# Moving ten convolution taps from GpSimd and ScalarE to VectorE in a two-layer decoder trunk

## The chip, the core and the metric

The kernel runs as one program on one NeuronCore of a Trainium2 chip. The number that counts is the device time of one execution in microseconds (us); lower is better. The engines go by their profile names: PE (matrix products) with PEld (its weight loads), DVE (VectorE), ACT (ScalarE), POOL (GpSimd) and SP (which issues most DMAs).

## What is computed

Two layers (`DEPTH = 2`) over 512 tokens of width 1024, in float32. Each layer is a half-weighted SwiGLU, a mixer, and a second half-weighted SwiGLU. The mixer is the part that matters here:

```python
h = rms_norm(x, mix_norm[l])
a, g, q, k, v = jnp.split(h @ w_in[l], splits, axis=-1)
conv_out = conv_module(a, g, conv_w[l], conv_b[l], conv_norm[l])
...
diff_out = diff_attention(q, k, v, rel_bias, lam, lam_init, subln_norm[l])
x = x + jnp.concatenate([conv_out, diff_out], axis=-1) @ w_out[l]

def conv_module(a, g, conv_w, conv_b, conv_norm):
    u = a * jax.nn.sigmoid(g)
    y = lax.conv_general_dilated(u, rhs, window_strides=(1,), padding=[(CONV_K - 1, 0)], ...)
    y = y + conv_b
    return jax.nn.silu(rms_norm(y, conv_norm))
```

The convolution is causal and depthwise: each of 512 channels is the weighted sum of 31 shifted copies of itself (`CONV_K = 31`). Its RMS norm runs over all 512 channels, so no channel can be finished before the sums of all of them are there. The attention has 4 heads with two softmax maps each, swept over four blocks of 128 queries.

## The kernel before

Activations lie feature-major: 128 features on the partitions, 512 tokens along the row. Large products are made of float32 parts, a rounded high part and the rest (`whi`/`wlo` for weights, `acth`/`actl` for activations), three products for each; ACT makes the high part of a weight (line 101) and DVE or POOL the rest (line 102).

`mixer` runs once per layer. Its 512 convolution channels are four tiles of 128, numbered 0 to 3. The order in which the source states the work is: the input projection of tiles 0 to 2 (`conv_in`), the query and key projections, tile 3's input projection, then two attention steps and the value projections, then `conv_taps(c, POOL_TAPS[c])` for the four tiles, then the other fourteen attention steps, then `conv_finish`, then the output projection. This order is a priority; a planner with its own costs for each instruction lays the final order of every engine at build time, and it may put later work ahead of earlier work that it does not see ready. On the chip each engine then runs its list in order.

`conv_taps(c, n)` makes tile `c`. The first `n` taps are ACT products (`prod`, line 916, two buffers) that POOL adds up one after the other (`yp`, lines 912 and 917); the others are DVE multiply-adds, each of which reads the running sum in a PSUM bank (`ps_y`) and one shifted slice of the input `u` in SBUF and writes the sum back (line 931). Where both have a share, DVE adds them (line 934). Then ACT squares the tile (`csq`, line 903; `csum`, line 900, for tile 0) and POOL adds the square to `csum` (line 904). Before the change tiles 0 and 2 are all DVE's (31 taps each), tile 1 is all POOL's and ACT's (31), and tile 3 is split: 10 to POOL and ACT, 21 to DVE.

```python
if n:
    yp = mp.tile([P, SEQ], F32, tag="yp%d" % (n < TAPS), name="yp")
    G.tensor_scalar(yp, us[c][:, 0:SEQ], ...)                        # line 912
    for t in range(1, n):
        p = mt.tile([P, SEQ], F32, tag="prod", name="prod")
        S.activation(p, us[c][:, t : t + SEQ], AF.Copy, scale=...)   # line 916
        G.tensor_tensor(yp, yp, p, op=ALU.add)                       # line 917
...
for t in range(n + 1 if n else 1, TAPS):
    V.scalar_tensor_tensor(ys[c] if last else y, us[c][:, t : t + SEQ], ..., y, ...)  # line 931
if n:
    V.tensor_tensor(ys[c], y, yp, op=ALU.add)                        # line 934
conv_square(c, ys[c])
```

`conv_finish` turns `csum` into one factor per token (PE transposes on line 267, DVE lines 271 and 272, POOL line 260, DVE line 289, PE line 293, ACT line 298), and for each tile runs POOL line 942, ACT 944, DVE 945, ACT 946, DVE 947. What it writes is the convolution half of the output projection's input.

An attention step is one head of one block of 128 queries; steps go from the last block (rows 512 wide) to the first (128 wide). `softmaxes` makes two score maps on PE (line 962, PSUM tags `sc` and `po`, two banks each), adds the bias and finds the maximum on DVE (line 966), takes the exponential on ACT (line 970), and combines the maps on DVE (lines 973, 975, 976). Two steps later `keys_first` transposes the map on PE (line 983) and copies it on ACT (line 985); one more step later `values` multiplies it with the values on PE (line 992). After four heads come a normalisation (lines 999 to 1007) and `block_out` (PE line 1019, ACT 1021, DVE 1022), which writes the attention half of the output projection's input. The output projection (lines 200, 203, 204, 1069) uses the tags `sc` and `po` too; it states the attention half for tokens 256 to 511 first, then the convolution half for all tokens, then the attention half for tokens 0 to 255. All 12 products of a 128-feature output need either the four convolution tiles or the attention blocks of their tokens.

Of the kernel before, what the change touches and what calls it, by code (L numbers as in the profile page):

```python
# [29 lines left out]
TAPS = 31  # L30
# [19 lines left out]
)  # L50
ORDER = (0, 4, 1, 5, 2, 6, 3, 7)

POOL_TAPS = (0, TAPS, 0, 10)


_COLS = [
# [14 lines left out]
def trunk(ctx: ExitStack, tc: tile.TileContext, xt, par, lamv, relb, onehot,  # L71
# [717 lines left out]
    def mixer(l, pr, after, begun):  # L789
        with tc.tile_pool(name="mix", bufs=1) as mp, tc.tile_pool(name="mt", bufs=2) as mt:  # L790
# [115 lines left out]
            def conv_taps(c, n):  # L906

                wc = _AT["conv_w"] + c * TAPS
                yp = None
                if n:  # L910
                    yp = mp.tile([P, SEQ], F32, tag="yp%d" % (n < TAPS), name="yp")
                    G.tensor_scalar(yp, us[c][:, 0:SEQ], pars[l][:, wc : wc + 1], col(l, "conv_b", c),
                                    op0=ALU.mult, op1=ALU.add)
                    for t in range(1, n):
                        p = mt.tile([P, SEQ], F32, tag="prod", name="prod")
                        S.activation(p, us[c][:, t : t + SEQ], AF.Copy, scale=pars[l][:, wc + t : wc + t + 1])  # L916
                        G.tensor_tensor(yp, yp, p, op=ALU.add)  # L917
                if n == TAPS:
                    ys[c] = yp
                    conv_square(c, yp)  # L920
                    return
                y = bank("y", "ps_y")
                if not n:
                    V.tensor_scalar(y, us[c][:, 0:SEQ], pars[l][:, wc : wc + 1], col(l, "conv_b", c),
                                    op0=ALU.mult, op1=ALU.add)
                else:
                    V.tensor_scalar(y, us[c][:, n : n + SEQ], pars[l][:, wc + n : wc + n + 1], None, op0=ALU.mult)
                ys[c] = us[c][:, PAD:]
                for t in range(n + 1 if n else 1, TAPS):
                    last = t == TAPS - 1 and not n  # L930
                    V.scalar_tensor_tensor(ys[c] if last else y, us[c][:, t : t + SEQ],
                                           pars[l][:, wc + t : wc + t + 1], y, op0=ALU.mult, op1=ALU.add)
                if n:
                    V.tensor_tensor(ys[c], y, yp, op=ALU.add)
                conv_square(c, ys[c])
# [116 lines left out]
            for c in range(CT):  # L1052
                conv_taps(c, POOL_TAPS[c])
            for n in range(2, len(steps) + 5):
# [139 lines left out]
```

## Time and profile before

| what | value |
|---|---|
| median of 3 runs | 1769.95 us (1769.82 to 1770.12) |
| profiled execution, its own time | 1770.11 us |
| its span in the profile | 1768.3 us (1.8 us lie outside it) |
| granted TensorE clock | 0.999 |
| mixer's convolution and attention, layer 0 | about 365 to 515 us of the span |
| the same in layer 1 | about 1243 to 1393 us |

"Busy" counts the time in which at least one instruction of an engine runs. PE matmuls are pipelined and their drawn ends reach into the next one, so PE can look busy across a short wait. In a timeline row the first number is the start, the second the length, "xN" the number of instructions merged into the row, and the brackets give the idle time before it and what ended it.

### The profile page before, as it was taken

The numbers are of one execution on the slowest core, as the hardware profiler recorded it, in microseconds if no ns is written. First come the engines' busy times: TensorE is split into PE (matmuls) and PEld (weight loads), VectorE is DVE, ScalarE is ACT, GpSimd is POOL, SyncE is SP. The second block draws the span as 40 slices with busy tenths as digits, with TensorE's granted clock in tenths as the row PEclk, the third lists the DMA queues.
The fourth block names the chain that finished last, engine by engine and source line by source line (L and its number), as shares of the span: only waits on it lengthen the run. The fifth ranks groups of instructions, "written<-read, shape, count | busy, mean of one in ns | idle before, by whom it ended". The sixth has DMA issues, their size and how long they took to land.

```text
span 1768.3 us, 32976 instructions
## 1 busy us (share of the span) xinstructions
PE 1757.9 (99%) x11852; PEld 1620.9 (92%) x11852; DVE 1474.8 (83%) x2655; ACT 1035.9 (59%) x1955; POOL 514.2 (29%) x497
## 2 busy tenths in 40 slices
PE   9999999999999999999999999999999999999998
PEld 7799999988788899999988999999887888999998
DVE  7969888987877969889987798899878678698887
ACT  6546566755855436566644565666559554465664
POOL 1011112169960011212200121121898600111122
PEclk9999999999999999999999999999999999999999
DMA  7457677533223457787544577776231335577775
GB/s 229 129 139 188 167 190 189 141 117 102 66 78 114 126 130 176 172 196 180 141 143 110 150 176 173 200 162 172 90 109 49 94 103 138 131 179 177 192 184 130
DMA packets 166613, 257.78 MB, mean 146 GB/s; under 512 B 19271, under 2 KB 63318, under 8 KB 166448
## 3 DMA queue, kind: packets, MB, share of 16 engines
q1 hardware_dynamic: 129600, 201.25, 36.3%
q0 software_dynamic: 36416, 54.12, 19.3%
q8 instruction: 93, 1.52, 0.4%
q14 instruction: 72, 0.59, 0.1%
q10 hardware_dynamic: 432, 0.29, 0.1%
HBM read 253.48 MB, written 3.42 MB: 145 GB/s over the span
## 4 chain that ended last, share of the span: by engine, by line
PE 93%; ACT 2%; POOL 1%; DVE 1%; DMA 0%; issue 0%; DVEq 0%; POOLq 0%; ACTq 0%
PE ps_pair L437 36%; PE ps_pair L526 18%; PE ps_pair L200 9%; PE ps_pair L203 9%; PE ps_pair L204 9%; PE ps_pair L845 2%; PE ps_pair L847 2%; PE ps_pair L846 2%; PE ps_out L200 2%; PE ps_out L203 2%; PE ps_out L204 2%; POOL yp L917 1%; ACT e L970 1%; ACT ps_sc L970 1%; ACT prod L916 0%; ACT at L985 0%
## 5 line engine op out<-in xcount | busy, mean ns | idle before, releaser
L101 ACT ACTIVATE whi<-wraw 128x512 fp32r<-128x512 f32 x744 | 453.2, 627 | 375.9 <-PE ps_pair L203 162.8
L102 DVE TENSOR_TENSOR wlo<-wraw,whi 128x512 fp32r<-128x512 f32 x640 | 426.2, 685 | 105.4 <-ACT whi L101 100.8
L160 POOL DMA_DIRECT2D wsum<-in_gu x128 | 111.9, 910 | 698.0 <-DMA wsum<-in_gu 291.9
L437 PE MATMUL ps_pair<-acth,wlo 128*128 128x256 f32 x1024 | 289.8, 283 | 0.0
L437 PE MATMUL ps_pair<-actl,whi 128*128 128x256 f32 x1024 | 289.8, 283 | 0.0
L437 PE MATMUL ps_pair<-acth,whi 128*128 128x256 f32 x1024 | 289.8, 283 | 0.0
L437 PE MATMUL ps_pair<-th,whi 128*128 128x256 f32 x768 | 217.3, 283 | 0.0
L437 PE MATMUL ps_pair<-tl,whi 128*128 128x256 f32 x768 | 217.3, 283 | 0.0
L437 PE MATMUL ps_pair<-th,wlo 128*128 128x256 f32 x768 | 217.3, 283 | 0.0
L203 PE MATMUL ps_pair<-actl,whi 128*128 128x512 f32 x512 | 199.7, 390 | 0.0
L200 PE MATMUL ps_pair<-acth,whi 128*128 128x512 f32 x512 | 199.0, 391 | 0.3 <-DVE gs L656 0.3
L204 PE MATMUL ps_pair<-acth,wlo 128*128 128x512 f32 x512 | 199.2, 390 | 0.0
L437 PEld LDWEIGHTS ps_pair<-actl,whi 128*128 128x128 f32 x1024 | 196.6, 192 | 0.2
L437 PEld LDWEIGHTS ps_pair<-acth,whi 128*128 128x128 f32 x1024 | 196.6, 192 | 0.2
L437 PEld LDWEIGHTS ps_pair<-acth,wlo 128*128 128x128 f32 x1024 | 196.6, 192 | 0.0
L160 POOL DMA_DIRECT2D wsum<-in_dn x112 | 98.8, 1107 | 271.2 <-ACT keep L442 51.0
L102 POOL TENSOR_TENSOR wlo<-wraw,whi 128x512 fp32r<-128x512 f32 x104 | 136.4, 1332 | 38.2 <-ACT whi L101 30.6
L437 PEld LDWEIGHTS ps_pair<-th,whi 128*128 128x128 f32 x768 | 147.5, 192 | 0.0
L437 PEld LDWEIGHTS ps_pair<-tl,whi 128*128 128x128 f32 x768 | 147.5, 192 | 0.0
L437 PEld LDWEIGHTS ps_pair<-th,wlo 128*128 128x128 f32 x768 | 147.5, 192 | 0.0
L526 PE MATMUL ps_pair<-hh,whi 128*128 128x256 f32 x512 | 144.9, 283 | 0.0
L526 PE MATMUL ps_pair<-hl,whi 128*128 128x256 f32 x512 | 144.9, 283 | 0.0
(210 smaller groups left out, 4448.8 us busy)
## 6 DMA issues: line engine op xcount, KB each, us to landing
wraw<-in_gu SPq DMA_DIRECT2D x280, 256.0 KB, 3.5
wsum<-in_gu SPq DMA_DIRECT2D x128, 256.0 KB, 3.8
wsum<-in_gu POOLq DMA_DIRECT2D x128, 256.0 KB, 4.9
wraw<-in_dn SPq DMA_DIRECT2D x68, 256.0 KB, 3.4
wraw<-in_wqkv SPq DMA_DIRECT2D x48, 256.0 KB, 2.8
wraw<-in_wout SPq DMA_DIRECT2D x48, 256.0 KB, 2.7
wraw<-in_dn SPq DMA_DIRECT2D x64, 128.0 KB, 3.9
wraw<-in_wag SPq DMA_DIRECT2D x32, 256.0 KB, 3.0
```

The costliest lines, as they stand in the source:

```text
L101: S.activation(hi, raw, AF.Copy)
L102: (eng or V).tensor_tensor(out=lo, in0=raw, in1=f32(hi), op=ALU.subtract)
L160: nc.gpsimd.dma_start(dst[:, to], src, accum_op=ALU.add)
L200: first = T.matmul(ps, wh, xh, start=start, stop=False)
L203: T.matmul(ps, wh, xl, start=False, stop=False)
L204: T.matmul(ps, wl, xh, start=False, stop=stop)
L437: mm = T.matmul(ps, l, r, start=first and i == j == 0, stop=False, skip_group_check=True)
L526: mm = T.matmul(ps, s[:, f], r, start=side not in self.begun, stop=False, skip_group_check=True)
L845: T.matmul(ps[n], xh[:, t], wh, start=k == 0, stop=False)
L846: T.matmul(ps[n], xh[:, t], wl, start=False, stop=False)
L847: T.matmul(ps[n], xl[:, t], wh, start=False, stop=k == KT - 1)
L970: S.activation(e, e, AF.Exp, bias=mn, scale=-1.0, accum_out=sm[:, m, h : h + 1])
```

## The change

Tile 3's ten POOL and ACT taps become DVE taps. Nothing else is edited. In each layer POOL loses one line-912 instruction and nine line-917 additions, ACT loses nine line-916 products, and DVE has 31 tap instructions for tile 3 (one line 924, thirty line 931) in place of 21 (one line 927, twenty line 931) and the addition of line 934. Tile 1 stays with POOL and ACT. The planner lays the order anew.

```diff
-POOL_TAPS = (0, TAPS, 0, 10)
+POOL_TAPS = (0, TAPS, 0, 0)
```

## The prediction

> **What bounds the kernel now.** I read the page's busy times and chain shares first.
>
> ```profile
> PE   1757.9 (99%) x11852; PEld 1620.9 (92%) x11852; DVE 1474.8 (83%) x2655; ACT 1035.9 (59%) x1955; POOL 514.2 (29%) x497
> PE 93%; ACT 2%; POOL 1%; DVE 1%; DMA 0%; issue 0%; DVEq 0%; POOLq 0%; ACTq 0%
> ```
>
> PE carries 93% of the chain that ended last, so over the whole kernel a change on the other engines can only win or lose what PE waits. The chain leaves PE for long only in the two mixers, so I asked for busy times by stretch there: first the time in which DVE runs tile 3's taps, then a gap on DVE, then the attention steps to the start of the output projection, then its first microseconds. Columns: stretch and its length, then PE, PEld, DVE, ACT, POOL busy.
>
> ```profile
> 443.44:464.22 20.78, 20.78 (x90) 15.98 (x89) 19.51 (x35) 15.96 (x31) 18.59 (x16) 1.00 0.09 27
> 464.22:466.49 2.27, 2.27 (x10) 1.54 (x9) 0.00 (x2) 2.27 (x5) 2.27 (x3) 1.00 0.22 75
> 466.49:475.00 8.51, 8.51 (x38) 5.18 (x37) 6.79 (x21) 7.76 (x21) 8.51 (x8) 1.00 0.44 136
> 475.00:485.00 10.00, 9.69 (x68) 8.26 (x66) 8.98 (x32) 9.97 (x30) 9.38 (x9) 1.00 0.26 79
> 485.00:495.30 10.30, 9.31 (x62) 7.51 (x63) 10.03 (x38) 7.74 (x28) 3.74 (x5) 1.00 0.01 2
> 495.30:505.00 9.70, 8.97 (x73) 8.63 (x72) 8.69 (x30) 8.78 (x24) 9.07 (x8) 1.00 0.09 28
> ```
>
> PE's visible idle in layer 0 is 0.31 + 0.99 + 0.73 = 2.03 us, all after 475. Up to 475 PE has no visible gap. From 475 to 485 ACT is full (9.97 of 10.00), from 485 to 495.3 DVE is (10.03 of 10.30). DVE's own idle is 1.27, 2.27, 1.72, 1.02 and 0.27 us in the first five stretches: 6.55 us in all. Layer 1 repeats this, so I work one layer out and double it:
>
> ```profile
> 1362.90:1373.20 10.30, 9.30 (x61) 7.50 (x62) 10.03 (x37) 7.74 (x27) 3.86 (x5) 1.00 0.01 2
> 1373.20:1382.90 9.70, 8.94 (x73) 8.63 (x72) 8.69 (x30) 8.78 (x25) 8.96 (x8) 1.00 0.08 27
> ```
>
> **What leaves POOL and ACT.** The rows of the tiles `u` and `yp` give count, then min/median/max in ns:
>
> ```profile
> L916 ACT ACTIVATE prod<-u,par x78: 704/722/746, 375.7 to 1359.9; 128x512 f32<-128x512 f32 x78
> L931 DVE SCALAR_TENSOR_TENSOR ps_y<-u,par,ps_y x156: 743/756/758, 369.7 to 1341.3; 128x512 f32<-128x512 f32 x156
> L934 DVE TENSOR_TENSOR u<-ps_y,yp x2: 680/680/681, 484.8 to 1362.8; 128x512 f32<-128x512 f32 x2
> L945 DVE SCALAR_TENSOR_TENSOR u<-th,u x6: 690/1337/1780, 498.5 to 1387.1; 128x512 f32<-128x512 f32 x6
> ```
>
> ```profile
> L917 POOL TENSOR_TENSOR yp<-yp,prod x78: 1266/1296/1337, 376.9 to 1361.0; 128x512 f32<-128x512 f32 x78
> L912 POOL TENSOR_SCALAR yp<-u,par x4: 770/782/817, 376.1 to 1323.2; 128x512 f32<-128x512 f32 x4
> ```
>
> POOL loses 9 x 1.30 + 0.78 = 12.5 us per layer, ACT loses 9 x 0.72 = 6.5 us. In the stretch where ACT is full, two things follow: attention's exponentials come sooner, and no product waits for a POOL buffer. Neither is worth anything by itself if DVE, which feeds ACT, has no time left. I therefore value the relief only as idle time that DVE can now fill. None of these instructions issues a DMA or is waited for by a queue that does, save POOL's weight splits of line 102, which move up.
>
> **What DVE gets.** The price of a tap depends on its neighbours:
>
> ```profile
> 452.78 0.75 DVE L931 SCALAR_TENSOR_TENSOR ps_y<-u,par,ps_y 128x512 f32<-128x512 f32 x1
> 453.44 0.69 DVE L966 CUSTOM_DVE_ANT_0 ps_sc<-ps_sc,bias 128x512 f32<-128x512 f32 x1
> ...
> 461.10 3.12 DVE L931 SCALAR_TENSOR_TENSOR ps_y<-u,par,ps_y 128x512 f32<-128x512 f32 x4
> 466.49 0.69 DVE L966 CUSTOM_DVE_ANT_0 e<-ps_sc,bias 128x512 f32<-128x512 f32 x1 [2.27 <-PE ps_sc L962]
> ...
> 471.39 0.75 DVE L976 SCALAR_TENSOR_TENSOR e<-ps_sc,c,e 128x512 f32<-128x512 f32 x1
> ...
> 484.80 0.68 DVE L934 TENSOR_TENSOR u<-ps_y,yp 128x512 f32<-128x512 f32 x1
> ...
> 494.56 0.74 DVE L1022 SCALAR_TENSOR_TENSOR actl<-ps_o,gsub,acth 128x512 fp32r<-128x512 f32 x1
> ```
>
> Taps that wait for each other step by (3.12 - 0.75) / 3 = 0.79 us; a tap with another instruction behind it takes 453.44 - 452.78 = 0.66 us. The twenty-first tap ends at 464.22, and DVE then stands for 2.27 us until PE has the next scores. Three of the ten new taps fit there (3 x 0.79 = 2.4). The other seven mix with the 512-wide attention steps, as taps did from 452 on: 7 x 0.66 = 4.6. Line 934 goes (0.68). DVE's net gain in work is 2.4 + 4.6 - 0.7 = 6.3 us per layer; the bounds are 10 x 0.66 - 0.68 = 5.9 and 10 x 0.79 - 0.68 = 7.2.
>
> Against it stand the idle times. The 2.27 us are filled whole. Of the 1.72 us to 475 DVE waits for scores that PE makes in its own time, so I credit half, 0.86. Of the 1.02 + 0.27 us to 495.3 some is waiting for ACT, which has lost products there; half again, 0.65. The 1.27 us before 464.22 lie ahead of the new taps and count nothing. Room: 3.8 us. So `block_out` of the second block, whose last instruction started at 494.56, comes 6.3 - 3.8 = 2.5 us late. Bounds: if all of the later idle time were used, 5.9 - 5.28 = 0.6; if only the gap, 7.2 - 2.27 = 4.9.
>
> PE's rows say who feels this:
>
> ```profile
> 474.59 0.60 PE L983 MATMUL ps_at<-ident,e 128*128 128x128 f32 x4
> ...
> 488.88 0.60 PE L267 MATMUL ps_rows<-ident,csum 128*128 128x128 f32 x4
> ...
> 495.65 0.36 PE L200 MATMUL ps_out<-acth,whi 128*128 128x256 f32 x1
> ...
> 498.69 0.39 PE L962 MATMUL ps_sc<-kt,qz 128*128 128x128 f32 x2
> ...
> 503.69 0.47 PE L200 MATMUL ps_out<-acth,whi 128*128 128x512 f32 x1 [0.73 <-DVE r L973]
> ```
>
> The third step's map was ready at 471.39 + 0.75 = 472.14 and PE transposed it at 474.59: 2.4 us of slack, which covers the early steps. In the narrow steps after 485 there is no such slack, since PE already stood still 0.99 us there. The output projection's first matmul, at 495.65, followed the `block_out` at once.
>
> **What moves with it.** Tile 3 was complete at 484.80 + 0.68 = 485.48. Its 31st tap should now end near 466.5 plus seven taps mixed with seven other instructions, 7 x (0.66 + 0.66) = 9.2, so near 476. `conv_finish` can start nine microseconds earlier. That has two sides. Its DVE instructions come into the fully used stretch before 495: I count two of the eight of lines 945 and 947 ahead of `block_out`, 2 x 0.69 = 1.4 us of further lateness (0.69 is line 945 at its shortest; at its longest, 1.78, it would be 3.6). And it hands PE convolution-half products while attention is slow: I credit the 0.73 us at 503.69 and the 0.99 us before 495.3. Per layer: 2.5 + 1.4 - 0.73 - 0.99 = 2.2 us lost. Twice that is 4.4 us on the profiled execution's 1770.11, so 1774.5; the median of the runs lies 0.16 below that execution, so 1774.3.
>
> [...]
>
> **The rivals.**
>
> First, **faster: the convolution half becomes PE's filler.** The chain of waits, in order of time, ran over POOL's taps and ACT's products into the attention steps:
>
> ```profile
> 458.59 2.56 POOL yp L917 x2
> ...
> 474.70 0.61 ACT prod L916
> ...
> 480.87 0.61 ACT prod L916
> ```
>
> If `conv_finish` is through by about 490, PE can work on the convolution half (8 outputs of twelve 512-wide matmuls each) whenever attention stalls. It decides if the first such matmul, at 503.69 before, starts before about 492. For it: tile 3 is ready nine microseconds sooner, and PE has 2.03 us of visible gaps, with more hidden under drawn matmul ends. Against it: `conv_finish` ranks behind the attention steps in the source, it needs a DVE that is full, and the output projection shares its four PSUM banks with scores, the last of which came only at 498.69. If the visible gaps go and half as much hidden time with them, the gain is near 2.5 us a layer (2.03 + 1.0, less 0.5 of early lateness): 1765. Both layers at twice the visible gap, 8 us, is the end I can see: 1762.
>
> Second, **no change worth measuring.** The slack of 2.4 us takes the lateness, ACT's relief lets DVE use all its later idle time, and the two sides of `conv_finish` cancel: 0.6 + 1.4 - 1.72 = 0.3 us a layer, 1770.5. Anything within 0.2%, 3.5 us, which is about what a measurement of this kernel can tell from no change, belongs here. That the taps lie wholly beside PE's work is the same case.
>
> Third, **the full price.** If DVE is the bound from 464 on and the planner's order wastes as much as it fills, all 6.3 us count in each layer: 1782.7.
>
> Fourth, **the taps run in one block ahead of the softmax.** They rank higher in the source. Then the next score map is read at 464.22 + 10 x 0.79 = 472.1 in place of 466.49, 5.6 us late, less 2.4 us of slack: 3.2 us of PE standing, with less of the later loss: about 1777.
>
> **How the numbers follow.** Forecast (slower, some 2 us a layer): 0.34. Block ahead of the softmax: 0.11. Full price: 0.05. No change: 0.21. Faster: 0.29. So faster by over 0.2%: 0.29, within: 0.21, slower: 0.50. The likeliest case's own range, from 1773.5 to 1779 (2.2 us moved by the bounds of 0.6 and 4.9 for 2.5), misses the faster side. The range of 8 in 10 goes from 1763, which keeps most of the faster case, to 1779.5, which leaves out the full price and the tail of the block case.
>
> **What would show it.** In the profile after: line 931 x174 to `ps_y` at 0.75 us, line 916 x60, line 917 x60, line 934 gone. DVE busy 12 to 13 us more, ACT about 13 us less, POOL about 25 us less. DVE without the 2.27 us gap at 464, and full from there to 495; ACT no longer full between 475 and 485. `conv_finish`'s transposes near 480 in place of 489. The forecast is right if PE stands longer between 466 and 497 and `block_out` comes two to three microseconds late; wrong if the first 512-wide output matmul comes before about 492, with PE's gaps gone, or if POOL's freed time moves something that I took as hidden, such as the output weights' splits.

## The result and the profile after

The changed kernel takes 1775.85 us (median of 8 runs, 1775.31 to 1776.12) against 1770.13 (8 runs) for the kernel before: ratio 1.0031, 95% interval 1.0020 to 1.0042, so 5.7 us slower. The profiled execution took 1775.31 us with a span of 1773.5, 5.2 us more than before in both.

The page after, in the lines that answer to those shown of before:

```profile
PE   1763.1 (99%) x11852; PEld 1623.4 (92%) x11852; DVE 1480.7 (83%) x2673; ACT 1024.7 (58%) x1937; POOL 486.2 (27%) x477
PE 96%; DVE 3%; ACT 0%; DMA 0%; issue 0%; POOL 0%; DVEq 0%
```

POOL lost 28 us of busy time and ACT 11; their shares of the chain that ended last fell from 1% and 2% to 0%, and DVE's rose from 1% to 3%. DVE gained only 6 us: far more busy time was freed than added, and the kernel still got slower.

Busy time by stretch, layer 0 (length, then PE, PEld, DVE, ACT, POOL, granted clock):

```profile
465.69:475.00 9.31, 9.29 (x43) 5.73 (x42) 8.62 (x24) 7.40 (x19) 7.28 (x6) 1.00 0.55 183
475.00:485.00 10.00, 9.59 (x63) 7.43 (x62) 9.86 (x33) 7.68 (x23) 2.92 (x4) 1.00 0.02 6
485.00:498.18 13.18, 11.54 (x66) 8.73 (x64) 12.92 (x44) 11.25 (x32) 6.61 (x7) 0.92 0.00 1
498.18:505.00 6.82, 6.82 (x54) 6.82 (x54) 6.62 (x20) 5.39 (x17) 2.58 (x2) 0.91 0.12 42
```

DVE is now full from 466 on. PE's visible idle is 0.02 + 0.41 + 1.64 = 2.07 us up to the first output matmul, against 0.31 + 0.99 before; the 0.73 us after it are gone. So the visible idle of the layer, 2.07 against 2.03 us, does not show the loss, though the first output matmul starts 2.53 us later (498.18 for 495.65). The third number from the end of a row is the granted clock; 1.00 throughout before, it is 0.92 and 0.91 in the last two rows here, and at half clock PE looks busy for longer with the same work (0.21 us from start to start of 128-wide matmuls in a row, 496.34 to 497.83, in place of 0.11, 502.15 to 502.71). The wait for ACT's copy that stood high in PE's list before is gone, and in the mixer nearly all that is left ends with DVE (both layers; total, times, longest; first before, then after):

```profile
PE ps_out L200 <- DVE r L973: 1.5, 2, 0.8
PE ps_o L992 <- ACT at L985: 1.5, 6, 0.3
...
PE ps_o L1019 <- DVE ov L1007: 1.0, 2, 0.5
```

```profile
PE ps_sc L962 <- DVE e L976: 1.6, 4, 0.5
PE ps_sc L962 <- DVE mn L966: 1.4, 2, 0.7
...
PE ps_at L983 <- ACT at L985: 0.4, 2, 0.2
```

The timeline of DVE, and below it of PE, shows the order that the planner chose:

```profile
466.38 0.69 DVE L966 CUSTOM_DVE_ANT_0 e<-ps_sc,bias 128x512 f32<-128x512 f32 x1 [0.69 <-PE ps_sc L962]
...
477.15 0.74 DVE L931 SCALAR_TENSOR_TENSOR u<-u,par,ps_y 128x512 f32<-128x512 f32 x1
...
490.99 1.32 DVE L945 SCALAR_TENSOR_TENSOR u<-th,u 128x512 f32<-128x512 f32 x1
...
493.65 0.74 DVE L947 SCALAR_TENSOR_TENSOR actl<-u,ghalf,acth 128x512 fp32r<-128x512 f32 x1
...
494.50 0.67 DVE L945 SCALAR_TENSOR_TENSOR yp<-th,yp 128x512 f32<-128x512 f32 x1
...
496.33 0.73 DVE L947 SCALAR_TENSOR_TENSOR actl<-yp,ghalf,acth 128x512 fp32r<-128x512 f32 x1
...
497.81 0.67 DVE L945 SCALAR_TENSOR_TENSOR u<-th,u 128x512 f32<-128x512 f32 x1
498.41 0.73 DVE L1022 SCALAR_TENSOR_TENSOR actl<-ps_o,gsub,acth 128x512 fp32r<-128x512 f32 x1
```

```profile
481.02 0.60 PE L267 MATMUL ps_rows<-ident,csum 128*128 128x128 f32 x4
...
498.18 0.58 PE L200 MATMUL ps_out<-acth,whi 128*128 128x256 f32 x1
...
506.28 0.48 PE L200 MATMUL ps_out<-acth,whi 128*128 128x512 f32 x1
```

The last tap ends at 477.9; `conv_finish` begins at 481 instead of 489; five of its eight instructions of lines 945 and 947 now lie ahead of the second `block_out`, none did before; that `block_out` starts 3.85 us late (498.41 for 494.56). And the convolution half, ready sooner, is used later: its first 512-wide matmul is at 506.28, before at 503.69.

Three theories could carry this. **Load**: DVE has ten more taps than idle time. **Order**: the early finish of the convolution takes DVE from the narrow attention steps. **Clock**: PE's waits set off a slower clock, and that is what costs.

### The profile page after: what moved, and what is told of

Its sections match the earlier page's. It is cut to its first block, busy times and chain, and to the rows that moved or that the text cites. A ratio compares the mean times of both kernels' runs of the same rounds, so it can differ in the third digit from the quotient of the medians.

```text
span 1773.5 us, 32940 instructions
## 1 busy us (share of the span) xinstructions
PE 1763.1 (99%) x11852; PEld 1623.4 (92%) x11852; DVE 1480.7 (83%) x2673; ACT 1024.7 (58%) x1937; POOL 486.2 (27%) x477
## 4 chain that ended last, share of the span: by engine, by line
PE 96%; DVE 3%; ACT 0%; DMA 0%; issue 0%; POOL 0%; DVEq 0%
PE ps_pair L437 36%; PE ps_pair L526 18%; PE ps_pair L200 9%; PE ps_pair L203 9%; PE ps_pair L204 9%; PE ps_out L200 2%; PE ps_out L203 2%; PE ps_out L204 2%; PE ps_pair L846 2%; PE ps_pair L845 2%; PE ps_pair L847 2%; PE ps_v L877 1%; PE ps_v L876 1%; PE ps_v L875 1%; PE ps_sc L962 1%; DVE ps_sc L966 0%
## 5 line engine op out<-in xcount | busy, mean ns | idle before, releaser
L102 POOL TENSOR_TENSOR wlo<-wraw,whi 128x512 fp32r<-128x512 f32 x104 | 132.8, 1292 | 56.7 <-ACT whi L101 53.1
L102 DVE TENSOR_TENSOR wlo<-wsum,whi 128x512 fp32r<-128x512 f32 x192 | 129.9, 683 | 18.1 <-ACT whi L101 18.1
```

The lines of the kernel that those rows point to most:

```text
L102: (eng or V).tensor_tensor(out=lo, in0=raw, in1=f32(hi), op=ALU.subtract)
```

## The experiments

Each time stands beside that of the kernel before on the same chip; differences are taken from that pair.

**Half the move** (`POOL_TAPS = (0, TAPS, 0, 5)`).

> Tile 3 gives POOL and ACT five taps in place of ten (before) or none (after). Three theories. Load: the loss is VectorE time beyond its idle time between 464 and 495; five more taps are 5 x 0.66 = 3.3 us a layer (line 934 stays) against 3.8 us of room, so no loss: 1770 to 1771.5 us. Order: the loss is the early finish of the convolution, whose VectorE instructions get ahead of the attention steps; tile 3 is then complete near 470, earlier than after, so most of the loss is there: 1774 to 1776. Clock: about half of the loss is the 3.41 us at clock 0.5 that the profile after shows once in each layer (495.98 and 1376.61), set off by PE's waits; without that stretch at most 1772, with it 1773 or more.

1772.94 against 1770.67: +2.3 us (1.0012, 1.0004 to 1.0021). This lies between the ranges of Load and Order, so it decides nothing alone; but its profile holds a natural test of the clock, used below.

**Relief without load**: tile 3's first ten taps left out of the sum.

```diff
-V.tensor_scalar(y, us[c][:, 0:SEQ], pars[l][:, wc : wc + 1], ...)
+f = 10 if c == CT - 1 else 0
+V.tensor_scalar(y, us[c][:, f : f + SEQ], pars[l][:, wc + f : wc + f + 1], ...)
...
-for t in range(n + 1 if n else 1, TAPS):
+for t in range(n + 1 if n else f + 1, TAPS):
```

> Tile 3's first ten taps are left out of the sum: POOL and ACT are relieved as after, VectorE has 21 taps and no line 934, so 0.7 us a layer less than before. Load: faster than before, by what the relief of ACT and POOL is worth and no more than PE's 2 us of visible waits a layer: 1766 to 1770, no stretch at clock 0.5. Order: the convolution is finished even earlier than after (tile 3 complete near 465), so the loss stays: 1773 to 1776.

1774.15 against 1770.67: +3.5 us (1.0022, 1.0013 to 1.0031). With less work on DVE, ACT and POOL than before, and the same on PE, the kernel is slower. Load cannot explain that. A stretch of this run, and DVE's timeline (lines are one higher than in the kernel before):

```profile
485.00:498.60 13.60, 10.00 (x65) 7.88 (x64) 13.60 (x46) 12.43 (x36) 5.17 (x7) 1.00 0.01 2
```

```profile
476.03 0.69 DVE L271 TENSOR_REDUCE rowv<-ps_rows 128x4 f32<-128x512 f32 x1
...
486.00 0.85 DVE L946 SCALAR_TENSOR_TENSOR u<-th,u 128x512 f32<-128x512 f32 x1
...
488.09 0.74 DVE L948 SCALAR_TENSOR_TENSOR actl<-u,ghalf,acth 128x512 fp32r<-128x512 f32 x1
...
496.78 0.73 DVE L948 SCALAR_TENSOR_TENSOR actl<-u,ghalf,acth 128x512 fp32r<-128x512 f32 x1
...
498.43 0.74 DVE L1023 SCALAR_TENSOR_TENSOR actl<-ps_o,gsub,acth 128x512 fp32r<-128x512 f32 x1
```

All eight finishing instructions lie ahead of the second `block_out`, and it comes as late as in the changed kernel. Up to the first output matmul DVE is full (13.60 of 13.60 us) and PE stands for 3.60 us, at full clock.

**Load without relief**: DVE makes all 31 taps, POOL and ACT their ten too, so ten taps are summed twice.

```diff
-V.tensor_scalar(y, us[c][:, n : n + SEQ], pars[l][:, wc + n : wc + n + 1], None, ...)
+V.tensor_scalar(y, us[c][:, 0:SEQ], pars[l][:, wc : wc + 1], None, ...)
...
-for t in range(n + 1 if n else 1, TAPS):
+for t in range(1, TAPS):
```

> VectorE makes all 31 taps of tile 3 and POOL and ACT make their ten as well, and line 934 adds them, so ten taps are counted twice. VectorE has its added load, ACT and POOL have no relief, and tile 3 is complete only when POOL is done, near 484 as before. Load: 7 us a layer more on VectorE than before, and ACT full at the same time: slower than after, 1776 to 1780. Order: the convolution is not finished early, so no loss: 1770 to 1772.

1772.86 against 1770.67: +2.2 us (1.0012, 1.0003 to 1.0021). Neither Load's range nor Order's holds this. The added DVE work costs something, but less than the change did, although nothing is relieved: the finish is late here (the second `block_out` starts at 498.24, the first line 945 at 499.89).

**Order undone**: the changed kernel, with its finishing instructions put behind the second `block_out`.

```diff
-V.scalar_tensor_tensor(cl[:, CT:, tq], pt, gsub[l], ...)
+written[i] = V.scalar_tensor_tensor(cl[:, CT:, tq], pt, gsub[l], ...)
...
-V.scalar_tensor_tensor(z, th, 1.0, z, op0=ALU.add, op1=ALU.mult)
+with behind(written[NT - 2]):
+    V.scalar_tensor_tensor(z, th, 1.0, z, op0=ALU.add, op1=ALU.mult)
```

> After, with the convolution's finishing instructions of line 945 on VectorE (and so those of 946 and 947) put behind line 1022 of the second attention block (tokens 256 to 383), as they lay before; five of them lay ahead of it after. Load: the ten taps alone cost 2.5 us of lateness a layer, less PE's waits that are filled: 1773 to 1777. Order: nothing of the loss is left: 1770 to 1771.5. Clock: if the stretch at clock 0.5 goes, 2 to 3 us of the 5.7 go with it: 1772.5 to 1774.

1771.22 against 1770.67: +0.55 us, and the interval holds no change (1.0003, 0.9995 to 1.0012). All taps are on DVE, and nine tenths of the loss are gone. Its timeline and stretch (lines one higher):

```profile
497.90 0.75 DVE L1023 SCALAR_TENSOR_TENSOR actl<-ps_o,gsub,acth 128x512 fp32r<-128x512 f32 x1
498.56 0.68 DVE L946 SCALAR_TENSOR_TENSOR u<-th,u 128x512 f32<-128x512 f32 x1
```

```profile
485.00:498.00 13.00, 12.50 (x82) 9.97 (x81) 12.40 (x56) 10.89 (x40) 6.60 (x7) 1.00 0.01 2
```

The second `block_out` is still 3.3 us later than before. But PE stands only 0.50 us in that stretch, against 1.64 us in a similar one of the changed kernel: 82 matmuls lie there, not 66. DVE has spent its time on attention steps, which PE can use, not on the convolution, whose first matmul PE starts only at 506.93 in this run. The hold moves ACT's line 946 with DVE's line 945, so the runs do not part the two engines; that DVE is the one that counts is read from its full rows and from PE's waits.

**Relief without load, order undone**: the second and the fourth edit together.

> The same ten taps of tile 3 left out as in the run with relief alone, and line 945 put behind line 1022 of the second attention block. Order: with the finishing instructions late and no added load nothing of the 3.5 us loss is left, and the relief shows: 1768 to 1770.7 us. Load: the order is nothing, so as without the hold: 1773.5 to 1775. The remainder against the held run with all taps (1771.2) is the price of the ten taps on VectorE when the order is right: order theory says 0.5 to 3 us for both layers.

1766.57 against 1770.66: -4.1 us (0.9978, 0.9969 to 0.9987), faster than either theory's range. In stretches:

```profile
475.00:485.00 10.00, 10.00 (x64) 8.06 (x64) 8.40 (x30) 7.82 (x24) 3.28 (x4) 1.00 0.17 50
485.00:494.40 9.40, 8.46 (x62) 7.01 (x60) 8.75 (x38) 8.19 (x28) 4.61 (x7) 1.00 0.00 0
494.40:505.00 10.60, 10.51 (x82) 9.94 (x82) 10.49 (x31) 9.13 (x27) 6.35 (x6) 1.00 0.16 53
```

So the corners are, in us against the kernel before:

| tile 3's first ten taps | finish as the planner lays it | finish held |
|---|---|---|
| on DVE (the change) | +5.7 | +0.55 |
| left out | +3.5 | -4.1 |

The early finish costs 5.2 us with the taps and 7.6 without; the ten taps on DVE cost 2.2 with the early finish and 4.6 without; the relief of POOL and ACT (with line 934's 1.4 us on DVE) is worth 4.1 where the order is right. Each corner's interval is some 2 us either way: both prices of the early finish and the 4.6 are clear of it, the 2.2 is not.

**The hold in the kernel before**, as a control.

> The kernel before with the same hold. In it line 945 lies behind line 1022 of the second block anyway (498.53 against 494.56), so the hold by itself should do nothing: 1770 to 1771. If it is faster or slower by more than 1 us, the hold has an effect of its own and the comparisons with it have to be read with that.

1770.46 against 1770.56: -0.1 us (1.0000, 0.9991 to 1.0009). The hold shows no effect of its own.

**Tile 3's input projection stated earlier**, in three kernels, to give DVE room.

```diff
 project(0, 0)
 to_features(1, 1)
+conv_in(CT - 1)
 project(0, 1)
 to_features(0, 0)
-conv_in(CT - 1)
 to_features(0, 1)
```

> After, with tile 3's input projection stated before the second half of the query projection, so that VectorE's 7.25 us gap at 432 to 439 holds taps and tile 3 is complete near 468 in place of 478. Load: VectorE is no longer short of time, 1766 to 1770. Order: the finishing instructions come some 10 us earlier still, near 480 to 490, ahead of the wide attention steps where PE has slack; if they are through before 488 and PE can fill its waits with the convolution half, 1766 to 1770; if they still lie among the narrow steps, 1772 to 1776.

> The same early input projection in the kernel before (ten taps of tile 3 with POOL and ACT). Tile 3's 21 taps on VectorE end near 455, but POOL still has both tiles' additions in one queue and finishes near 484, so the convolution is finished when it was. Load: VectorE has 7 us more room in the attention steps, 1767 to 1770. Order: same finish, same order, 1769.5 to 1771.5.

> After with the early input projection and with line 945 behind line 1022 of the second attention block. Load: 1766 to 1770 as without the hold. Order: the taps are out of the way before the attention steps and the finishing instructions come after the second block, so at or below the kernel before: 1767 to 1770.5; if the run without the hold is faster than this one, an early finish helps once VectorE has room, and it was the crowding with the taps, not the early finish as such, that cost time.

All three theories missed: 1787.55, 1781.50 and 1777.97 against 1770.66 (1.0097, 1.0058 and 1.0043, the lowest interval from 1.0030). The first one's stretch at the place of the edit shows a part of why:

```profile
440.00:445.00 5.00, 2.17 (x7) 1.66 (x6) 4.89 (x9) 4.67 (x9) 5.00 (x5) 0.78 0.53 159
```

PE is left 2.8 us without work there, with waits for `qz` from ACT that the old order hid (`PE ps_v L875 <- ACT qz L891`, 5.7 us in two times; 4.9 and 5.7 us in the other two runs). The edit brought waits of its own, and the runs say little on load. Among them the hold is again worth 9.6 us (1787.55 to 1777.97).

**Half the move, order undone**, and with seven taps.

> Five taps of tile 3 with POOL and ACT, and line 945 behind line 1022 of the second attention block. From the four corners (relief -4.1 us, load +4.6, early finish +5 to +7.6): if load and relief go with the number of taps and the first taps fall into idle time, half of each and less of the load: 1768 to 1770.5, better than both kernels. If the load is all paid, 1770.5 to 1771.5.

> Seven taps with POOL and ACT, with the same hold. If the first moved taps are free because they fall into VectorE's 2.27 us gap at 464, while POOL and ACT lose three taps: 1768 to 1770. If what counts is when POOL is done with tile 3, as before: 1770 to 1771.5.

Five taps: 1769.07 against 1770.56, -1.5 us (0.9992, 0.9983 to 1.0001). Seven: 1770.30, -0.3 us (0.9996, 0.9987 to 1.0005). Held, the times over ten, seven, five and no taps on POOL are -0.1, -0.3, -1.5 and +0.55: lowest at five, but by less than the intervals, so a minimum is not shown. It is the lowest median of the kernels that compute the whole sum, but its interval just reaches 1; I call it no worse than before, not shown to be faster.

**Filling PE's waits.** In the changed kernel the clock record shows one stretch of 3.41 us at 0.5 in each layer (from 495.98 and from 1376.61). Layer 0 in steps of 3 us:

```profile
490.00:493.00 3.00, 2.72 (x16) 1.77 (x14) 2.96 (x8) 2.70 (x10) 3.00 (x3) 1.00 0.00 0
493.00:496.00 3.00, 1.64 (x10) 1.20 (x10) 3.00 (x12) 2.96 (x11) 1.42 (x3) 1.00 0.00 0
496.00:499.00 3.00, 3.00 (x16) 2.62 (x14) 3.00 (x10) 2.49 (x8) 0.00 (x0) 0.50 0.03 8
```

PE works 1.64 of 3.00 us, and the next stretch runs at half clock. The test repeats the transposes of the 256-wide attention steps:

```diff
-T.transpose(pt[:, t], maps[i, h][:, t], ident)
+for _ in range(2 if i == 1 else 1):
+    T.transpose(pt[:, t], maps[i, h][:, t], ident)
```

> After, with the transposes of line 983 made twice for the 256-wide steps: eight more of 0.11 us a layer, 0.9 us of PE work a layer, laid among PE's waits between 484 and 496. Clock: PE counts as busier, the stretch at clock 0.5 goes, and the time falls by up to 1.5 us against after (the layers of the run with five taps differ by 0.75 us, one with that stretch and one without): 1774 to 1775.5. If PE's waits for VectorE alone set the time, the fill changes nothing or adds up to 1.8 us: 1775.7 to 1777.6.

1776.06 against 1770.56: +5.5 us (1.0030, 1.0018 to 1.0041), no different from the change, with 1.8 us of PE work added. The slow stretch of layer 0 is gone, and the granted clock of the whole profiled run is 0.999, in the changed kernel 0.998; layer 0:

```profile
493.00:496.00 3.00, 2.12 (x14) 1.52 (x12) 3.00 (x13) 2.79 (x9) 2.29 (x3) 1.00 0.00 0
496.00:499.00 3.00, 2.48 (x17) 2.06 (x18) 3.00 (x12) 2.87 (x8) 0.00 (x0) 1.00 0.03 8
```

At full clock PE stands visibly for 0.52 us of the second row, where at half clock it looked busy throughout: the slow stretch covered waits. So the slow clock has a small price: by the medians, between the 0.2 us by which the two differences differ and 2.0 us, if all of the filler's 1.8 us were paid; the differences have intervals of some 2 us either way, so these bounds are rough. The run with five taps and no hold points the same way: its layer 0 has the slow stretch (0.50 from 496 to 499) and its layer 1 not (1.00 from 1367 to 1379), and from the first value projection to the start of the last output matmul they take 106.92 and 106.17 us, 0.75 us apart; the same two stretches are 105.23 and 105.39 in the kernel before. And relief alone lost 3.5 us with no such stretch inside (granted clock of its profiled run 1.000).

## Why the prediction was right, and where its working was not

The forecast of 1774.3, in a range of 1763.0 to 1779.5, met 1775.85; slower came true. By its own steps:

- **Counts and prices held.** Line 931 x174 and line 916 x60 came, taps kept their price, and line 934 is gone. DVE's busy time grew by 5.9 us, not by my 12 to 13, partly because line 945 ran at its short length nearly throughout (its median for `u` fell from 1337 to 682 ns, 2.3 us less in all for its eight instructions). In both layers the one long instruction that is left, 1.3 us, lies beside POOL's line 942 (at 490.99 and 1371.60, line 942 from 490.67 and 1371.28 for 2.59); but before the change one of 0.68 us (502.54) lay beside POOL work too (line 102, from 502.63 for 1.73), so that POOL's smaller share is the cause is not shown:

```profile
L931 DVE SCALAR_TENSOR_TENSOR ps_y<-u,par,ps_y x174: 742/756/757, 369.6 to 1356.2; 128x512 f32<-128x512 f32 x174
L916 ACT ACTIVATE prod<-u,par x60: 707/724/747, 375.5 to 1338.0; 128x512 f32<-128x512 f32 x60
L945 DVE SCALAR_TENSOR_TENSOR u<-th,u x6: 672/682/1323, 491.0 to 1381.6; 128x512 f32<-128x512 f32 x6
```

- **The placing of the taps held.** I said three (two came) fill the gap at 464 and the others mix with attention one for one; the last ended at 477.9 for my 476. They did not run in one block.
- **The lateness held, its parts and its meaning did not.** I forecast 2.5 + 1.4 = 3.9 us at the second `block_out`; 3.85 came. But I took lateness from the taps as loss. The held run has 3.3 us of lateness and loses 0.3 us a layer, because PE goes on with attention meanwhile. The term "2.5 us lost a layer" is that 0.3, in which the relief of POOL and ACT is counted.
- **The term for `conv_finish` had the wrong sign.** I put 1.4 us against 0.73 + 0.99 us given back, a gain of 0.3 a layer. Undoing the order gives 2.6 us a layer (5.2 in both). I counted two finishing instructions ahead of `block_out` where five came, and credited PE with early convolution products that it did not take: 506.28 for 503.69. The visible 0.73 us went, but brought nothing back: from the first output matmul to the first 512-wide one PE needs 8.10 us, before 8.04, with 48 output matmuls in both.
- **The relief of ACT and POOL was undervalued.** I gave it nothing beyond DVE's idle time; the corner without load shows 4.1 us for both layers, though 1.4 us less DVE work is in it.

So 2.2 us a layer was near the 2.9 measured because too much load (2.5 for 0.3, net of relief) stood against too little order (-0.3 for 2.6). The direction and the place came from the rows, DVE's lateness ahead of the second `block_out`; that the sum came out near was luck. The lower end of the likeliest case's own range, 1773.5, did not follow from its bounds either: 2.2 - 1.9 = 0.3 us a layer gives 1770.5, which is the second rival. The kernel with all taps on DVE and the finish held, DVE at 84%, is level with the one before, DVE at 83% (1.0003, 0.9995 to 1.0012): DVE's busy share does not rank the two here.

What stays open: why the planner puts the early finish among the narrow steps, since its own costs are not in the profile; and whether filling PE with finished convolution tiles could be made to pay, since the earliest such matmul of any run started at 502.64, in the held run with relief.

## What to carry to other kernels

When an edit lets a side chain finish sooner, ask what its last instructions now stand in front of: work that becomes ready early can cost more than the work that was moved. Cross the two suspects (do the work or not, hold the order or not) before trusting a sum that comes out right; here two wrong terms made a total that was nearly right. And lateness of one product is a loss only if the bound engine has nothing else to do until it comes.

## What the runs showed of the hardware

In the changed kernel the granted clock of PE fell to 0.5 for 3.41 us in each layer (from 495.98 and from 1376.61), with no PE wait longer than 1.0 us from one matmul's start to the next in the 3.41 us before. At half clock 128-wide matmuls in a row step by 0.21 us (496.34 to 497.83) in place of 0.11 (502.15 to 502.71). PE was not idle before it: it was busy 2.04 of the 3.41 us.

Nor does that busy share sort the stretches. The first of the two below, of the changed kernel, with 2.04 us, was followed by half clock; the second, of the run with relief alone, with 1.98 us, by full clock (granted clock of that run 1.000):

```profile
492.57:495.98 3.41, 2.04 (x11) 1.48 (x12) 3.41 (x12) 3.37 (x11) 1.85 (x3) 1.00 0.00 0
```

```profile
1372.89:1376.30 3.41, 1.98 (x13) 1.63 (x14) 3.41 (x12) 2.67 (x8) 1.01 (x1) 1.00 0.00 0
```

With the transposes of the 256-wide steps made twice, layer 0 showed no stretch at 0.5 (1.00 from 490 to 502). What sets the change off is not shown beyond that.
